# Three edits of order in a tuned encoder layer: earlier last products in a transition, a later copy of v, and P4 ahead of P3

## The chip, the cores and the metric

The kernel runs on one core of a Trainium2 chip. The metric is the device time of one execution in microseconds (us). Engines are named as in the profile: PE is TensorE's matmuls and PEld its weight loads, DVE is VectorE, ACT ScalarE, POOL GpSimd, SP SyncE (which here only issues DMAs).

## What is computed

One layer of an encoder trunk on 1024 tokens of width 1024, in float32: two half-step SwiGLU blocks of hidden width 2816, and between them a mixer that projects into two attentions (a 2-D neighbourhood attention with 8 heads, and a windowed attention with rotary embedding, 8 query heads on 2 key heads), gates their outputs and adds the result.

```python
h = x + 0.5 * swiglu(rms_norm(x, n1), wg1, wu1, wd1)
u = rms_norm(h, nm)
qa, ka, va, qb, kb, vb, ga, gb = split(u @ w_in)
ya = neighbourhood_attention_2d(qa, ka, va, rpb)
yb = windowed_gqa_sink(rope(qb), rope(kb), vb, sink)
h = h + (sigmoid(ga) * (ya @ wa) + sigmoid(gb) * (yb @ wb)) @ wo
h = h + 0.5 * swiglu(rms_norm(h, n2), wg2, wu2, wd2)
y = rms_norm(h, nf)
```

## The kernel before

**Numbers.** Every float32 operand of a big product is split into a high and a low part (`split`, L92: a cast on ACT at L93, a subtraction on DVE at L94), and each product is three matmuls, high by high, high by low, low by high (`mm3`, L145, L147, L149). In the weights' preparation the same two steps stand at L308 (ACT) and L311 (DVE).

**Strassen's scheme.** The big products are done by a seven-product scheme (P1 to P7). Of the right-hand sides, `to_strassen` (L189) turns each of eight token tiles by eight transposes on PE (L138, in `turned`) and puts parts of it into the blocks B11 and B21 (tiles 0 to 3), and T1, T2, B22 (tiles 4 to 7, with sums on DVE at L209 to L215). `strassen_rest` (L221) adds T3 and T4. P4 multiplies T4, and P3 multiplies B22.

**`products` (L233)** runs the seven products of n groups, each in two halves m = 0 and 1, in the order of a list `seq`: P1 and P2 of the first groups, then group by group P5, P6, P7, P3, P4. One product here is 4 column blocks of 3 matmuls, so 12 matmuls. `prep_until` prepares the weights of the product up to eight places ahead. Of group i and half m, P1, P6, P7 and P4 add into one PSUM bank W, P2 goes to X, and P5 and P3 add into Y. After each product the running sum in its bank is read: `after` is called at once behind it. Then `at_end(k)` runs with k, the number of products that are left, and calls whatever is hooked to that k.

**The projections** are `products` with five groups of four chunks of 128 columns (`groups`, L875), 70 products in all, and `store_z` (L879) as `after`: it reads the bank on ACT (L911) where nothing is to be added, and else on DVE (L913), and for P2, P7, P3 and P4 has POOL store the result, to z_d (L891), to g_d (L893), or split to zs_d (L889). The tiles that it writes are a ring of eight in the tensor `fa`. `at_end` runs the hooks of L1034 to L1044, named by the number of products left:

- `rope` (L923), five times at 48, 45, 42, 39 and 36: SP loads a chunk from z_d twice (L931, L934), DVE makes three operations of it (L935 to L937), POOL stores it to zr_d (L938). It takes two tiles `xs`, of which there are two in all.
- `v_b` (L947, at 30) loads v into an `xs` tile; `order_v` (L952, at 28) copies it on ACT in another order into a second `xs` tile (L954); `turn_v` (at 16) transposes it on PE.
- `q_b` and `k_b` (at 7, 6 and 4) split q and k; `gate_first` (at 2) loads the first gate's weights; `keep_u` (L994, at 0) loads the kept part of u (L999) and splits it into the two halves of T4's tile, where the gates behind the projections read it.

**The transition (`transition`, L161)** joins a stage of eight output tiles to the next stage. For each tile t there is `pre(t)`, which for t of 4 and above is `Down.tail(t - 4)` (L623): the last entries of the product P4 of the stage before, 5 entries of 3 matmuls in the first transition and 4 of 3 in the second; then an eviction on DVE (L601) and a store of the tile from SP (L920, L1435). Then `normed` (L116: square on ACT L123, two small steps on POOL L126 and L127, a scaling on DVE L129), then `to_strassen`, then `post`, which from tile 3 on lets the next stage's `products` go on by 30 matmuls. It is called in two halves of four tiles. In the second half the order is: pre(4), pre(5), norm 4; then with tile 4: pre(6), norm 5, turn 4, post; with tile 5: pre(7), norm 6, turn 5, post; and so on. There are two transitions, from the first SwiGLU into the projections (near 580 to 690 us of the trace) and from the mixer into the second SwiGLU (near 1265 to 1330 us).

**What sets the order.** Outside the first stage, which is laid out by hand, the program text gives each instruction a priority by its place, and a planner fixes each engine's order before the run: by its own estimates of durations it gives an engine the first instruction in the text whose inputs and tiles are ready. So an instruction can stand on its engine earlier or later than the text has it, and on the chip each engine then keeps to that fixed order.

**After the projections** attention begins: `scores` (L1268) writes a sink column (L1282) and a softmax (L1283 on DVE, L1286 and L1291 on ACT) into tiles that lie over the ring in `fa`, so it waits until the results there are stored; `turn` transposes them on PE (L1299). Between them PE is filled with the gates' matmuls (`gate`, L1116), which read T4's tile from their fifth block on.

Of the kernel before, what the change touches and what calls it, by code (L numbers as in the profile page):

```python
# [15 lines left out]
P = 128  # L16
# [20 lines left out]
def trunk_kernel(ctx, tc, x, xt, n1, wg1, wu1, wd1, nm, win, rpb, sink, wa, wb, wo,  # L37
# [35 lines left out]
    def new_ar(g, dt=F32R):  # L73
        ar[g] = main.tile([P, 4, 1024], dt, tag=f"ar{g}", bufs=1, name=nm_("ar"))
        return ar[g]
# [28 lines left out]
    def w_cols(w, c0, n=P):  # L104
        return w[:, c0:c0 + n].rearrange("(c p) f -> p c f", p=P)
# [10 lines left out]
    def normed(h, gb, xs=None, parts=1):  # L116

        xs = xs4() if xs is None else xs
        w = D // parts
        cols = [slice(i * w, (i + 1) * w) for i in range(parts)]  # L120
        st = const.tile([P, 4], F32, tag="st", bufs=4, name=nm_("st"))
        for i, c in enumerate(cols):
            nc.scalar.activation(xs[:, c], h[:, c], AF.Square, scale=D ** -0.5, accum_out=st[:, i:i + 1])  # L123
        if parts == 2:
            nc.gpsimd.tensor_tensor(st[:, 0:1], st[:, 0:1], st[:, 1:2], op=ALU.add)
        nc.gpsimd.tensor_scalar(st[:, 0:1], st[:, 0:1], EPS, None, op0=ALU.add)  # L126
        nc.gpsimd.tensor_tensor(st[:, 2:3], st[:, 0:1], nhalf, op=ALU.pow)  # L127
        for c in cols:
            nc.vector.scalar_tensor_tensor(out=xs[:, c], in0=h[:, c], scalar=st[:, 2:3], in1=gb[:, c],  # L129
                                           op0=ALU.mult, op1=ALU.mult)  # L130
        return xs
# [29 lines left out]
    def transition(pre, gain, turn_tile, post, halves=1):  # L161

        h, xs = {}, {}
        n = NTT // halves
        for base in range(0, NTT, n):
            for t in (base, base + 1):
                h[t] = pre(t)
            xs[base] = normed(h.pop(base), gain)
            yield
            for t in range(base, base + n):  # L170
                if t + 2 < base + n:
                    h[t + 2] = pre(t + 2)
                if t + 1 < base + n:
                    xs[t + 1] = normed(h.pop(t + 1), gain)
                turn_tile(t, xs.pop(t))
                if t:
                    post(t - 1)
                yield
        post(NTT - 1)
# [50 lines left out]
    PRODUCTS = ("P1", "P2", "P5", "P6", "P7", "P3", "P4")  # L230
    RIGHT = dict(P1=B11, P2=B21, P6=T2, P5=T1, P7=T3, P3=B22, P4=T4)

    def products(src, n, after, at_end, extra, ring, by_hand=False):  # L233

        seq = [(i, p, m) for i in range(n) for p in PRODUCTS for m in range(2)]  # L240
        early = [(i, p, m) for i in (range(2, 5) if by_hand else range(3)) for p in ("P1", "P2") for m in range(2)]
        if by_hand:
            early = [(i, p, m) for p in ("P2", "P1") for i in range(2) for m in range(2)] + early
# [1 line left out]
        seq = early + [s for s in seq if s not in early]  # L245
# [141 lines left out]
    def behind(prods):  # L387

        run, load_ahead = prods[2:4]

        def post(t):
            if t >= 3:
                drain(run, 10)
            if t in (3, 4):
                load_ahead(t - 2)

        return post

    def hidden(wg, wu, at_end, ring=(8, 9, 10, 11), by_hand=False):
# [16 lines left out]
        def after(i, p, m, bks, snap, sn):  # L416
# [47 lines left out]
            else:  # L464
# [10 lines left out]
                if p != "P3":  # L475
# [10 lines left out]
            yield  # L486

        return products(lambda i, m, half: (wg, wu)[m][i + half * NP], NP, after, at_end, (6, 7),
                        [*ring, *range(8)], by_hand)

# [384 lines left out]
    groups = [[(12, 13), (14, 15)], [(16, 17), (0, 1)], [(4, 5), (8, 9)], [(2, 3), (6, 7)], [(10, 11), (18, 19)]]  # L875
    NG = len(groups)
# [154 lines left out]
    def hook(n, *f):  # L1031
        hooks.setdefault(n, []).append(f)
# [2 lines left out]
        hook(14 * (NG - 1) - 8 - 3 * c, rope, c)  # L1035
    hook(14 * (NG - 2) - 6, rope, 4)
    hook(14 * (NG - 2) - 12, v_b)
    hook(14 * (NG - 2) - 14, order_v)
    hook(14 * (NG - 3) - 12, turn_v)
    hook(7, q_b, 0)  # L1040
    hook(6, k_b)
    hook(4, q_b, 1)
    hook(2, gate_first)
    hook(0, keep_u)  # L1044
    pg = products(lambda i, m, half: w_cols(win[0], groups[i][m][half] * P), NG, store_z, at_end, (2, 3), range(8, 16))
    down.into(transition(down1, gain, to_strassen, behind(pg), 2), pg)
    kept.clear()
    strassen_rest()
# [317 lines left out]
    t = new_ar(2, F32)  # L1366
# [65 lines left out]
    def down2(t):  # L1432
# [3 lines left out]
        return res(t)  # L1436

    merge.into(transition(down2, gain, to_strassen, behind(hg), 2), hg)
    strassen_rest()
    drain(hg[2])  # L1440
# [116 lines left out]
```

## Time and profile before

| | before |
|---|---|
| median of 3 runs | 1935.5 us |
| lowest and highest run | 1934.52 and 1937.35 us |
| span of the profiled execution (its first to its last instruction) | 1934.8 us |
| instructions | 25499 |
| busy: PE | 1922.2 us |
| busy: DVE | 1437.1 us |
| busy: ACT | 943.6 us |
| busy: POOL | 295.5 us |

The page and the trace are of one profiled execution. Beside its span it has no other time of its own; the timed runs are separate ones. A row of the timeline has the start in us from the span's start, the duration in us, the engine, the line, the operation, what it writes and reads, the shape, how often, and in brackets how long the engine had been idle before and what released it. SPq is SP's queue: the rows are DMA issues. Matmuls overlap: each shows 0.39 us, but they follow one another by less.

### The profile page before, as it was taken

How to read it: one execution, taken by the hardware profiler on the slowest of the kernel's cores; microseconds unless marked ns; L12 is line 12 of the kernel's file. 1: busy time of each engine (PE TensorE's matmuls, PEld its weight loads, DVE VectorE, ACT ScalarE, POOL GpSimd, SP SyncE). 2: the span in 40 equal slices, each digit the busy share in tenths (PEclk: the TensorE clock that was granted, in tenths of full speed). 3: DMA queues.
4: the chain of work that ended last, by engine and by line, in shares of the span. 5: the costliest groups of instructions: out<-in, count | busy, mean ns of one | idle time of the engine just before them, and what ended most of it. 6: DMA issues, size and time to landing. Idle time of an engine off the chain costs nothing.

```text
span 1934.8 us, 25499 instructions
## 1 busy us (share of the span) xinstructions
PE 1922.2 (99%) x8956; PEld 1603.1 (83%) x8956; DVE 1437.1 (74%) x2560; ACT 943.6 (49%) x1827; POOL 295.5 (15%) x432
## 2 busy tenths in 40 slices
PE   9999999999999999999999999999999999999998
PEld 7888888888888888888888888878888888888886
DVE  7987765668957788678888857889676566569864
ACT  6532333344446543477877862365333333344453
POOL 0011110013300112211122231010111001005210
PEclk9999999999999999999999999999999999999999
DMA  6344323286234478553458576533423323493341
GB/s 261 100 167 163 129 104 128 86 289 225 88 109 137 159 223 250 185 163 104 116 134 195 184 242 210 169 140 133 147 87 109 126 87 109 140 355 104 112 144 61
DMA packets 151745, 298.70 MB, mean 154 GB/s; under 512 B 14912, under 2 KB 64448, under 8 KB 151616
## 3 DMA queue, kind: packets, MB, share of 16 engines
q1 hardware_dynamic: 123072, 210.53, 33.6%
q0 software_dynamic: 27824, 85.48, 13.3%
q8 instruction: 71, 1.16, 0.3%
q10 hardware_dynamic: 720, 1.05, 0.1%
q14 instruction: 58, 0.48, 0.1%
HBM read 210.50 MB, written 88.27 MB: 154 GB/s over the span
## 4 chain that ended last, share of the span: by engine, by line
PE 88%; issue 7%; POOL 1%; DMA 1%; DVE 1%; ACT 1%; POOLq 0%; SPq 0%; ACTq 0%; DVEq 0%
PE g L149 16%; PE g L147 16%; PE g L145 16%; PE d L149 11%; PE d L147 11%; PE d L145 11%; PE d L1299 2%; PE g L1313 1%; PE g L1318 1%; PE d L1278 1%; PE d L1279 1%; POOL zs_d L889 1%; PE d L138 1%; POOL z_d L891 1%; DMA zr_d<-xs 0%
## 5 line engine op out<-in xcount | busy, mean ns | idle before, releaser
L145 PE MATMUL g<-ar,ws 128*128 128x512 f32 x1128 | 423.1, 395 | 0.6 <-ACT fa L911 0.6
L147 PE MATMUL g<-ar,ws 128*128 128x512 f32 x1128 | 417.2, 390 | 0.9 <-DVE ar L94 0.5
L149 PE MATMUL g<-ar,ws 128*128 128x512 f32 x1128 | 416.1, 390 | 0.2 <-DVE ws L311 0.2
L145 PE MATMUL d<-ar,ws 128*128 128x512 f32 x736 | 282.4, 391 | 0.3 <-ACT ar L810 0.2
L147 PE MATMUL d<-ar,ws 128*128 128x512 f32 x736 | 281.9, 390 | 0.3 <-DVE ar L812 0.3
L149 PE MATMUL d<-ar,ws 128*128 128x512 f32 x736 | 281.6, 390 | 0.5 <-DVE ws L311 0.5
L147 PEld LDWEIGHTS g<-ar,ws 128*128 128x128 f32 x1128 | 211.8, 188 | 46.2 <-DVE ar L94 1.0
L149 PEld LDWEIGHTS g<-ar,ws 128*128 128x128 f32 x1128 | 211.7, 188 | 45.5 <-DVE ws L311 0.7
L145 PEld LDWEIGHTS g<-ar,ws 128*128 128x128 f32 x1128 | 206.4, 188 | 37.8 <-ACT fa L911 1.0
L311 DVE TENSOR_TENSOR ws<-raw,ws 128x512 fp32r<-128x512 f32 x204 | 139.6, 690 | 99.6 <-ACT ws L308 98.8
L308 ACT CAST ws<-raw 128x512 fp32r<-128x512 f32 x204 | 125.1, 620 | 140.6 <-PE g L149 64.4
L145 PEld LDWEIGHTS d<-ar,ws 128*128 128x128 f32 x736 | 138.3, 188 | 29.7 <-ACT ar L810 0.6
L147 PEld LDWEIGHTS d<-ar,ws 128*128 128x128 f32 x736 | 138.4, 188 | 29.6 <-DVE ar L812 0.6
L149 PEld LDWEIGHTS d<-ar,ws 128*128 128x128 f32 x736 | 138.4, 188 | 29.4 <-DVE ws L311 0.7
L93 ACT CAST ws<-raw 128x512 fp32r<-128x512 f32 (+1 forms) x121 | 81.0, 669 | 144.0 <-PE d L149 61.8
L94 DVE TENSOR_TENSOR ws<-raw,ws 128x512 fp32r<-128x512 f32 (+1 forms) x119 | 93.7, 789 | 59.8 <-ACT ws L93 59.3
L414 POOL DMA_DIRECT2D hid<-fx x91 | 49.3, 542 | 431.5 <-DVE fx L474 304.9
L93 ACT CAST ar<-raw 128x512 fp32r<-128x512 f32 (+1 forms) x83 | 56.0, 679 | 94.8 <-PE g L147 55.0
L94 DVE TENSOR_TENSOR ws<-ar,ws 128x512 fp32r<-128x512 f32 x114 | 98.3, 867 | 3.8 <-ACT ws L93 3.7
L145 PE MATMUL g<-ws,ws 128*128 128x512 f32 x232 | 91.0, 392 | 0.0
L149 PE MATMUL g<-ws,ws 128*128 128x512 f32 x232 | 90.5, 390 | 0.0
L147 PE MATMUL g<-ws,ws 128*128 128x512 f32 x232 | 90.3, 389 | 0.0
(313 smaller groups left out, 3607.4 us busy)
## 6 DMA issues: line engine op xcount, KB each, us to landing
raw<-hid SPq DMA_DIRECT2D x70, 512.0 KB
hid<-fx POOLq DMA_DIRECT2D x91, 256.0 KB, 2.4
ar<-in_ffn_w_down_dram SPq DMA_DIRECT2D x32, 512.0 KB
raw<-in_ffn_w_up_dram SPq DMA_DIRECT2D x31, 512.0 KB
raw<-in_ffn_w_gate_dram SPq DMA_DIRECT2D x27, 512.0 KB
raw<-in_w_in_dram SPq DMA_DIRECT2D x27, 512.0 KB
hid<-fa POOLq DMA_DIRECT2D x51, 256.0 KB, 2.7
ar<-zs_d POOLq DMA_DIRECT2D x48, 256.0 KB, 5.3
```

The costliest lines, as they stand in the source:

```text
L93: nc.scalar.copy(dst_hi, src)
L94: (eng or nc.vector).tensor_tensor(dst_lo, src, f32v(dst_hi), op=ALU.subtract)
L138: nc.tensor.transpose(pt[:, c * P:(c + 1) * P], xs[:, (half * 4 + c) * P:(half * 4 + c + 1) * P], ident)
L145: nc.tensor.matmul(b, lhs[0], r[0], start=first, stop=False, **kw)
L147: nc.tensor.matmul(b, lhs[0], r[1], start=False, stop=False, **kw)
L149: nc.tensor.matmul(b, lhs[1], r[0], start=False, stop=last, **kw)
L308: nc.scalar.copy(w[0][:, :512], a)
L311: nc.vector.tensor_tensor(w[0][:, 512:], a, f32v(w[0][:, :512]), op=ALU.subtract)
L414: nc.gpsimd.dma_start(hid[PRODUCTS.index(p), i], src)
L889: nc.gpsimd.dma_start(d[ch * P:(ch + 1) * P, cols], t)
L891: nc.gpsimd.dma_start(z_d[ch * P:(ch + 1) * P, cols], c)
L1299: nc.tensor.transpose(pt[:, i * P:(i + 1) * P], un["pr"][s][:, i * P:(i + 1) * P], ident)
```

## The change

Three edits:

1. In `transition`, in the second half of the tiles, pre(6) and pre(7) both come with tile 4, ahead of norm 5 and of tile 4's transposes; pre(7) came with tile 5. It holds in both transitions.
2. The hook of `order_v` moves from 28 products left to 24.
3. `products` takes the order of the seven as an argument, and the projections have P4 ahead of P3; `keep_u` is hooked to 1 product left in place of 0. The second SwiGLU's and the first one's products keep their order.

```diff
@@ transition
             for t in range(base, base + n):
-                if t + 2 < base + n:
-                    h[t + 2] = pre(t + 2)
+                for k in (t + 2, t + 3) if base and t == base else (t + 2 + (base > 0),):
+                    if k < base + n:
+                        h[k] = pre(k)
                 if t + 1 < base + n:
                     xs[t + 1] = normed(h.pop(t + 1), gain)
                 turn_tile(t, xs.pop(t))
@@ products
-    def products(src, n, after, at_end, extra, ring, by_hand=False):
+    def products(src, n, after, at_end, extra, ring, by_hand=False, order=PRODUCTS):
-        seq = [(i, p, m) for i in range(n) for p in PRODUCTS for m in range(2)]
+        seq = [(i, p, m) for i in range(n) for p in order for m in range(2)]
@@ the projections
-    hook(14 * (NG - 2) - 14, order_v)
+    hook(14 * (NG - 2) - 18, order_v)
-    hook(0, keep_u)
-    pg = products(lambda i, m, half: w_cols(win[0], groups[i][m][half] * P), NG, store_z, at_end, (2, 3), range(8, 16))
+    hook(1, keep_u)
+    pg = products(lambda i, m, half: w_cols(win[0], groups[i][m][half] * P), NG, store_z, at_end, (2, 3), range(8, 16),
+                  order=("P1", "P2", "P5", "P6", "P7", "P4", "P3"))
```

## The prediction

> **What bounds the kernel now.** I read the page's first part, then the waits of TensorE, then the timeline around each of those waits on every engine.
>
> ```profile
> span 1934.8 us, 25499 instructions
> PE 1922.2 (99%) x8956; PEld 1603.1 (83%) x8956; DVE 1437.1 (74%) x2560; ACT 943.6 (49%) x1827; POOL 295.5 (15%) x432
> ```
> ```profile
> PE d L138 <- DVE xs L129: 0.8, 1, 0.8
> PE g L145 <- ACT fa L911: 0.6, 1, 0.6
> PE g L147 <- DVE ar L94: 0.5, 1, 0.5
> PE d L149 <- DVE ws L311: 0.5, 1, 0.5
> ```
>
> The reader is to see how little there is to win. PE is busy for 99% of the span, and the change removes no matmul. These four waits (of 0.8, 0.6, 0.5 and 0.5 us) are all the waits of 0.5 us and more behind the first stage's start, 2.4 us together. The first three lie where the change edits. So the question is whether an edit moves a wait off PE's path without laying a new one on it. A wait costs a little more than the idle time shown: I count from start to start, against the pace of undisturbed matmuls, which the two PE rows of group 0 below give: twelve from 698.67 to 701.39, 0.227 us each.
>
> **Edit 1: tile 7's last products before tile 4's transposes.** This happens in both transitions. In the second one:
>
> ```profile
> 1289.16 0.39 PE L149 MATMUL g<-ws,ws 128*128 128x512 f32 x1
> 1290.35 1.06 PE L138 MATMUL d<-ident,xs 128*128 128x128 f32 x8 [0.80 <-DVE xs L129]
> 1295.59 0.50 PE L149 MATMUL g<-ar,ws 128*128 128x512 f32 x1 [0.24 <-DVE ws L311]
> 1301.43 0.40 PE L149 MATMUL g<-ws,ws 128*128 128x512 f32 x1
> 1315.96 0.50 PE L149 MATMUL d<-ar,ws 128*128 128x512 f32 x1 [0.48 <-DVE ws L311]
> ```
> ```profile
> 1293.65 1.29 DVE L129 SCALAR_TENSOR_TENSOR xs<-fa,st,gain 128x1024 f32<-128x1024 f32 x1 [0.79 <-POOL st L127]
> ```
> ```profile
> 1300.00:1305.00 5.00, 5.00 (x28) 4.21 (x27) 4.99 (x9) 4.87 (x10) 0.51 (x2) 1.00 0.38 126
> ```
>
> The transposes of tile 4 were due at 1289.16 + 0.23 = 1289.39 and began at 1290.35: 0.96 us lost, because tile 4's norm on DVE came late. Tile 7's last products are 4 entries of 3 matmuls, 12 x 0.227 = 2.72 us, and they depend on nothing of the norm. Put in front, they more than fill the gap, and that wait goes. What is late next is DVE. In the window (columns: busy PE, PEld, DVE, ACT, POOL, then clock, DMA) the third busy figure, DVE's, is 4.99 of 5 us, and the wait at 1315.96 already ends with a DVE subtraction of the next stage's weights (L311). Whatever PE gains before 1316 it can keep only as far as DVE gets earlier too. DVE's idle time that this can fill is the 0.79 at 1293.65: the weight tiles come free when tile 7's products have read them, so their conversion can start earlier. I take **-0.8**, nearest to that row. The ends: -1.7 (0.96 + 0.24 + 0.48, if DVE keeps up), and +0.9. The second end because the planner, which orders each engine's instructions by its own estimates, had laid some of tile 7's matmuls among the next stage's (the one at 1301.43 is the last of them); four such fillers gone are 4 x 0.227 = 0.9 us of PE with nothing beside the wait at 1295.59.
>
> Moved with these products go one eviction on DVE and one store of tile 7 on SP's queue, which now precedes weight loads:
>
> ```profile
> 1303.08 0.33 SPq L1435 DMA_DIRECT2D h_d<-fa  x1
> ```
>
> 0.33 us of SP, which waits for nothing there; I cost it at nothing. The first transition:
>
> ```profile
> 642.00 0.39 PE L149 MATMUL g<-ar 128*128 128x512 f32 x1
> 642.23 1.03 PE L138 MATMUL d<-ident,xs 128*128 128x128 f32 x8
> 660.00:670.00 10.00, 10.00 (x54) 8.47 (x53) 10.00 (x17) 7.58 (x14) 1.08 (x2) 1.00 0.49 167
> ```
>
> Here the transposes follow without a gap, so nothing is won. Five entries, 15 x 0.227 = 3.4 us, go ahead of them, and DVE gets tile 4's work 3.4 us later before a stretch in which it is full (10.00 of 10). Idle DVE time later in the tiles covers that; without the cover up to 1 us could return in group 0. Value 0, ends 0 and +1.0.
>
> **Edit 2: P4 ahead of P3.** P6, P7 and P4 add into the same PSUM bank (W); after each, the running sum is read. Between P7 and P4 stood P3, in another bank (Y). Now P4 of half 0 starts one product (2.72 us) after P7 of half 0 ends, and waits until DVE has read that bank. This is the change's added wait, and group 0 shows where it bites:
>
> ```profile
> 698.67 0.39 PE L145 MATMUL d<-ar,ws 128*128 128x512 f32 x1
> 701.39 0.39 PE L145 MATMUL d<-ar,ws 128*128 128x512 f32 x1
> ```
> ```profile
> 696.50 0.69 DVE L315 TENSOR_TENSOR s<-fx 128x512 f32<-128x512 f32 x1 [5.20 <-DMA fx<-in_w_in_dram]
> 699.14 0.69 DVE L913 SCALAR_TENSOR_TENSOR fa<-g,fa 128x512 f32<-128x512 f32 x1
> 703.36 0.68 DVE L913 SCALAR_TENSOR_TENSOR fa<-g,fa 128x512 f32<-128x512 f32 x1
> ```
>
> The PE rows are the starts of the two products behind P7, P3's halves before and P4's after. DVE stands 5.20 us for a weight load and then works off what piled up, so it has read P7's two banks only at 699.14 + 0.69 = 699.83 and 703.36 + 0.68 = 704.04. If all orders stay, P4's first half starts 699.83 - 698.67 = 1.16 us late, the second at 704.04 in place of 701.39 + 1.16 = 702.55, 1.49 late: **2.65 us**. Behind the waiting matmul stands all of PE. Against it: the planner lets a ready product go first where it foresees a wait, as it did with tile 7's matmuls, and P3's inputs are ready. Ends 0 and 2.65; nothing in the trace says which is nearer, so I take the middle, **+1.3**. In the other groups I expect P7's bank to be read in time. In group 3 DVE already stands waiting for P7:
>
> ```profile
> 789.53 0.69 DVE L913 SCALAR_TENSOR_TENSOR fa<-g,fa 128x512 f32<-128x512 f32 x1 [0.58 <-PE g L149]
> ```
>
> 0.69 us of reading fits into the 2.72 of P7's other half. What could break it is a wait of DVE for a rope load, 2.0 us at the longest:
>
> ```profile
> DVE xs L935 <- DMA xs<-z_d: 4.5, 4, 2.0
> ```
>
> 2.0 + 0.69 just fits; with one more operation like the 1.23 us subtraction quoted in edit 4 it is 1.2 over. Value 0, ends 0 and +1.2. P4's own evict is on ACT, P3's on DVE; both only change places, as do the two raw tiles that their preparation frees for SP's loads.
>
> **Edit 3: v's copy.**
>
> ```profile
> 786.43 0.50 PE L145 MATMUL g<-ar,ws 128*128 128x512 f32 x1 [0.56 <-ACT fa L911]
> ```
> ```profile
> 784.84 1.05 ACT L954 COPY xs<-xs 128x1024 f32<-128x1024 f32 x1 [3.26 <-DMA zr_d<-xs]
> 785.79 0.59 ACT L911 ACTIVATE fa<-g 128x512 f32<-128x512 f32 x1
> ```
> ```profile
> 705.53 0.54 POOL L891 DMA_DIRECT2D z_d<-fa  x1 [0.66 <-DVE fa L913]
> ```
> ```profile
> 707.97 0.34 SPq L931 DMA_DIRECT2D xs<-z_d  x1
> ```
>
> ACT stood at v's copy for 3.26 us until the last rope's store had left the tile it writes, then copied for 1.05, and P6's evict behind it came after; P7 on PE lost 0.72 us start to start. The hook's new place alone does little: the copy was already some six products past its hook, held by the store. But P3 of group 0 comes two products later, so the store at 705.53 and the first rope load at 707.97 come 2 x 2.72 = 5.4 us later, and the five ropes run one behind the other through two buffers, so the copy moves to about 784.84 + 5.4 = 790.2. P6's two evicts are then past, and the next evict on ACT is P4's, near 786.43 + 3 x 2.72 = 794.6. **-0.7**; ends -0.7 and, if the copy lands before P6's second evict and waits as long, +1.5.
>
> **Edit 4: T4's split one product earlier.**
>
> ```profile
> 849.02 0.40 PE L147 MATMUL g<-ar,ws 128*128 128x512 f32 x1
> 849.95 0.50 PE L147 MATMUL g<-ar,ws 128*128 128x512 f32 x1 [0.53 <-DVE ar L94]
> 850.75 0.60 PE L1299 MATMUL d<-ident,fa 128*128 128x128 f32 x4
> ```
> ```profile
> 844.84 0.15 DVE L1282 COPY fa<-nsk 128x1 f32<-128x1 f32 x1 [3.78 <-DMA z_d<-fa]
> 845.29 0.15 DVE L1282 COPY fa<-nsk 128x1 f32<-128x1 f32 x1 [0.30 <-DMA g_d<-fa]
> 846.57 0.48 DVE L1283 CUSTOM_DVE_ANT_0 fa<-d,masks,nsk 128x256 f32<-128x256 f32 x1
> 848.67 1.23 DVE L94 TENSOR_TENSOR ar<-raw,ar 128x1024 fp32r<-128x1024 f32 x1
> ```
> ```profile
> 850.00 0.51 ACT L1291 ACTIVATE fa<-fa,rc 128x256 f32<-128x256 f32 x1 [0.87 <-DVE fa L1282]
> ```
>
> P4 was T4's last reader and the last product, so T4 could be refilled only after it. With P3 last, T4 is free 5.4 us earlier, and the split (its last part at 848.67 here) is done before the first gate needs it: 849.95 - 849.02 - 0.23 = 0.7 us won, **-0.7**. The two loads of u that feed it are long issued:
>
> ```profile
> 836.25 1.81 SPq L999 DMA_DIRECT2D raw<-u_d  x2
> ```
>
> so the earlier hook moves ACT's and DVE's parts alone, and no queue of DMAs. The upper end is the rival below.
>
> Sum: -0.8 + 0 + 1.3 + 0 - 0.7 - 0.7 = **-0.9 us**. The profiled execution shows a span of 1934.8; the median of the three runs is 1935.5, 0.7 above it, the margin around the span. So 1934.8 - 0.9 + 0.7 = **1934.6 us**. 0.2% is 3.9 us, about what a measurement of this kernel can tell from no change: I forecast within that.
>
> **Rivals.** *No wait in group 0* (chance 0.22): the planner puts P3's matmuls where P4 would wait. For it speaks that it has done so with tile 7's; against it that its estimate did not foresee DVE's 5.20. Then -2.2, 1933.3.
>
> *First softmax behind P3's store, slower* (0.17): the sink copies of attention's second unit need the buffers of P3's results stored. DVE stood at them until 845.29, ahead of the first unit's softmax at 846.57. P3's store now issues 5.4 us later, less the time its evict had waited. The store's landing:
>
> ```profile
> DMA to landing us min/median/max: 5.4/5.7/6.1
> ```
>
> P3 would end with PE's last projection matmul near 842, its store issue near 843 and land by 849.1. From DVE's release to the first unit's scaled rows took 850.00 + 0.51 - 845.29 = 5.22 us, so 854.3, where PE comes to its transposes at 850.75: +3.6 in place of -0.7. If the two T4 subtractions (1.23 each) now fit into the wait, 851.9, +1.1. It decides as soon as the copies stand ahead of that softmax in DVE's order. I set +2.4 for edit 4: -0.9 + 3.1 = +2.2, 1937.7. A sentence aside: the Trainium skill, page "DMA: Bandwidth & Descriptors", section "Anatomy of one DMA", gives a DMA 2.0 us plus its bytes at 436 GB/s, by which a 256 KB store would land in 2.6 us and this rival would be nearly void; the rows here, with other transfers under way, are twice that, and I go by the rows.
>
> *v's copy blocks another evict* (0.08): edit 3 gives 0 in place of -0.7, 1935.3.
>
> *The waits slow PE's clock, slower* (0.05). PE's granted clock is 1.00 in the windows above, but not everywhere:
>
> ```profile
> 16.00:19.30 3.30, 3.30 (x11) 2.53 (x11) 1.13 (x2) 0.87 (x2) 0.79 (x1) 0.50 1.03 408
> ```
>
> Early in the first stage, behind thin work, it is 0.50 for 3.3 us, half of which is lost: 1.65. Group 0's two waits, 2.65 us within 5.4, could bring the same: 1.35 (the full waits) + 1.65 - 0.9 = +2.1, 1937.6. For it speaks that row; against it that 0.96 us at 1290 left the clock alone. The Trainium skill, page "TensorE: Matmul & The Clock Gate", section "Part 1: The HAM clock gate", lets the clock fall to half after an idle window of about 3.4 us; by that rule waits of 1.16 and 1.49 us cost only themselves, and neither wait of before is long enough to test it.
>
> **How the numbers follow.** Forecast 0.48, rivals 0.22, 0.17, 0.08, 0.05. Low: no wait in group 0 (-2.2) with edit 1 at its end of -1.7 gives -3.1: 1932.4. High: the slower rival at 1937.7 with a little more of group 0's wait: 1938.2. Nearly all cases lie within 0.2%: faster by more than that needs every edit at its good end and something unnamed besides, 0.05; slower by more needs the slower rival with group 0's full wait or the slow clock, 0.11; the same 0.84.
>
> **What would show it.** In the profile after: no wait of L138 on L129 in the second transition, and DVE still full with a PE wait on L311 near 1315; a wait of L145 on DVE's L913 near 700 (up to 1.2 and 1.5); v's copy near 790 with no evict behind it; no wait on L94 near 849, and L1283 ahead of the second unit's L1282. I am wrong if PE waits on L1299 after the projections, or if the planner's order differs far from the edits.

## The result and the profile after

The changed kernel took 1938.87 us (median of 21 runs, 1937.33 to 1940.65), the kernel before 1936.25 us beside it (21 runs, 1934.52 to 1939.16): a ratio of 1.0014, 95% interval 1.0007 to 1.002. So the change costs 2.6 us, where 0.9 us of gain was forecast; the time lies above the range that was given. The profiled execution of the changed kernel has a span of 1937.1 us, 2.3 above that of before.

The page's first part, for the changed kernel:

```profile
span 1937.1 us, 25490 instructions
PE 1921.8 (99%) x8956; PEld 1602.9 (83%) x8956; DVE 1435.4 (74%) x2560; ACT 944.5 (49%) x1827; POOL 293.8 (15%) x432
```

Nothing is to be learned from it: PE is busy for 99% in both, with the same 8956 matmuls. The waits of PE tell more (engine, tile, line, what ended the wait: total, times, longest), from 575 to 1345 us of the changed kernel. Its lines behind `transition` are one further down than those of before, from about 1050 on two.

```profile
PE g L145 <- ACT fa L912: 2.9, 1, 2.9
PE g L145 <- DVE fa L914: 1.5, 2, 1.0
PE d L1301 <- issue: 0.5, 1, 0.5
PE d L145 <- DVE ar L94: 0.2, 1, 0.2
```

All four waits of before are gone or changed. The two of the second transition (L138 on L129, L149 on L311) have vanished, T4's (L147 on L94) too; the one on ACT's evict has grown from 0.6 to 2.9 us, and 1.5 us on DVE's evict are new.

To see what each place is worth, I counted every matmul from start to start and took off the 0.227 us per 512 columns of the undisturbed pace. What is left, in us, by stretch of the span:

| stretch | before | after | after - before |
|---|---|---|---|
| 0 to 640 (first stage, first transition's start) | 11.97 | 10.81 | -1.16 |
| 640 to 700 (first transition, group 0) | 2.27 | 3.97 | +1.71 |
| 700 to 770 (groups 0 to 2) | -0.01 | 0.80 | +0.81 |
| 770 to 830 (groups 3 and 4) | 1.35 | 5.25 | +3.90 |
| 830 to 870 (end of the projections) | 3.01 | 2.21 | -0.80 |
| 870 to 1265 (attention) | 26.41 | 27.11 | +0.70 |
| 1265 to 1345 (second transition) | 6.75 | 3.93 | -2.82 |

The sum is +2.3, the difference of the spans. The first and the sixth row are scatter: these stretches hold the same TensorE work in the same order in every kernel here, and over all fourteen profiles they lie between 10.3 and 12.4 and between 26.1 and 28.3. The first row's scatter has a visible cause: in the profile of before the granted clock was 0.50 for 3.4 us near 16 us, as the prediction shows, and in that of the changed kernel it was 1.00 there. The six profiles with this slow stretch have 11.6 to 12.4 in the row, the eight without it 10.3 to 10.9. The second row has some scatter in it too: five profiles of kernels with the old order there, that of before and four of the experiments, have 2.3 to 3.4 in it, the seven with the new first transition 3.9 to 4.2. The rest I put down to the change.

**Where it went: 770 to 830.** PE and ACT there, from the timeline of the changed kernel (start, duration, engine, line, operation, tiles, shapes; in brackets the idle time before it and what ended that):

```profile
792.86 0.52 PE L145 MATMUL g<-ar,ws 128*128 128x512 f32 x1 [2.91 <-ACT fa L912]
793.60 0.63 PE L149 MATMUL g<-ar,ws 128*128 128x512 f32 x1
794.02 0.63 PE L145 MATMUL g<-ar,ws 128*128 128x512 f32 x1
...
796.58 0.42 PE L145 MATMUL g<-ar,ws 128*128 128x512 f32 x1
```
```profile
784.60 0.60 ACT L912 ACTIVATE fa<-g 128x512 f32<-128x512 f32 x1 [1.68 <-PE g L149]
785.09 0.61 ACT L309 CAST ws<-fx 128x512 fp32r<-128x512 f32 x1
791.26 1.04 ACT L955 COPY xs<-xs 128x1024 f32<-128x1024 f32 x1 [5.56 <-DMA xs<-z_d]
792.21 0.59 ACT L912 ACTIVATE fa<-g 128x512 f32<-128x512 f32 x1
```

Read ACT's rows from top to bottom: P6's first evict, a cast, then v's copy, which waits 5.56 us for its tile, and only behind it P6's second evict. In the kernel before the copy (784.84) stood ahead of both: P6's first evict followed at 785.79, and the second here:

```profile
786.79 0.60 ACT L911 ACTIVATE fa<-g 128x512 f32<-128x512 f32 x1
```

The second evict's bank is the one that P7's second half adds into, so PE stands for 2.91 us. The second thing to see is in PE's starts: from 793.60 on they are 0.42 us apart and not 0.23, until 796.58. The windows of the changed kernel (columns: busy PE, PEld, DVE, ACT, POOL, then PE's granted clock, DMA share, GB/s):

```profile
789.90:792.90 3.00, 0.09 (x2) 0.05 (x1) 0.00 (x0) 1.64 (x3) 0.00 (x0) 1.00 0.22 89
793.20:796.60 3.40, 3.40 (x10) 2.62 (x9) 3.18 (x5) 1.25 (x3) 0.53 (x1) 0.50 0.53 159
796.80:800.20 3.40, 3.40 (x16) 2.78 (x15) 2.07 (x3) 1.25 (x2) 1.35 (x3) 1.00 0.46 142
```

Behind the wait the granted clock is 0.50 for 3.4 us, with 10 matmuls in place of 16, though PE counts as busy all through. Eight starts are 0.2 us late each, 1.6 us. So the copy costs 3.08 (the wait, from start to start) + 1.6 = 4.7 us, less the 0.72 that the wait at 786 had cost before.

**Why the copy is late.** The first rope load and the last rope's store of the changed kernel (SP's queue, POOL):

```profile
711.62 0.34 SPq L932 DMA_DIRECT2D xs<-z_d  x1
783.62 0.53 POOL L939 DMA_DIRECT2D zr_d<-xs  x1 [2.94 <-DVE xs L938]
```

In the kernel before they stand at 707.97 and, by its timeline, at 777.64: the rope chain starts 3.7 us later and ends 6.0 us later.

**The new waits on DVE.** In the first transition and in group 2 of the changed kernel:

```profile
660.98 0.50 PE L145 MATMUL g<-ar,ws 128*128 128x512 f32 x1 [1.01 <-DVE fa L914]
748.84 0.47 PE L145 MATMUL g<-ar,ws 128*128 128x512 f32 x1 [0.45 <-DVE fa L914]
```
```profile
660.24 1.28 DVE L914 SCALAR_TENSOR_TENSOR fa<-g,fa 128x512 f32<-128x512 f32 x2
745.67 1.22 DVE L936 TENSOR_TENSOR xs<-xs,fx 128x1024 f32<-128x1024 f32 x1 [4.05 <-DMA xs<-z_d]
746.81 0.68 DVE L914 SCALAR_TENSOR_TENSOR fa<-d,hs 128x512 f32<-128x512 f32 x1
```

At 660 DVE, without a gap since 648.48, is still at the tiles' work that came to it later (tile 4's third sum, L215, at 651.49; before, at 646.00), and reads group 0's banks late. At 745 it stood 4.05 us for a rope load; before, the longest such wait was 2.0 us.

**What was won.** In the second transition of the changed kernel no wait of PE is left (1265 to 1345 us). The first of the three windows there from 1300 to 1315, and PE at the end of the projections:

```profile
1300.00:1305.00 5.00, 5.00 (x24) 4.09 (x23) 5.00 (x8) 3.88 (x7) 0.54 (x1) 1.00 0.76 285
```
```profile
855.60 0.63 PE L1301 MATMUL d<-ident,fa 128*128 128x128 f32 x4 [0.47 <-issue]
```

DVE's busy time (the third figure) is 5.00 of 5 in all three windows, a little more than before, and PE waits for it nowhere. At the end of the projections the wait for T4's split is gone, and a wait of 0.47 us ahead of the first unit's transposes has come.

### The profile page after: what moved, and what is told of

The parts are those of the page before. It is cut to its first block, busy times and chain, and to the rows that moved or that the text cites. A ratio compares the mean times of both kernels' runs of the same rounds, so it can differ in the third digit from the quotient of the medians.

```text
span 1937.1 us, 25490 instructions
## 1 busy us (share of the span) xinstructions
PE 1921.8 (99%) x8956; PEld 1602.9 (83%) x8956; DVE 1435.4 (74%) x2560; ACT 944.5 (49%) x1827; POOL 293.8 (15%) x432
## 3 DMA queue, kind: packets, MB, share of 16 engines
q8 instruction: 71, 1.16, 0.2%
## 4 chain that ended last, share of the span: by engine, by line
PE 90%; issue 6%; POOL 1%; DVE 1%; ACT 1%; DMA 1%; POOLq 0%; SPq 0%; ACTq 0%; DVEq 0%
PE g L145 17%; PE g L147 17%; PE g L149 17%; PE d L149 11%; PE d L147 11%; PE d L145 11%; PE d L1301 2%; PE g L1320 1%; PE d L1280 1%; PE g L1315 1%; PE d L1281 1%; PE d L138 1%; POOL zs_d L890 1%; POOL z_d L892 0%; DMA fx<-in_xt_dram 0%
## 5 line engine op out<-in xcount | busy, mean ns | idle before, releaser
L147 PE MATMUL g<-ar,ws 128*128 128x512 f32 x1128 | 417.5, 391 | 0.4 <-DVE ar L834 0.4
L149 PE MATMUL g<-ar,ws 128*128 128x512 f32 x1128 | 417.1, 390 | 0.0
L147 PE MATMUL d<-ar,ws 128*128 128x512 f32 x736 | 281.6, 390 | 0.6 <-DVE ar L813 0.6
L149 PE MATMUL d<-ar,ws 128*128 128x512 f32 x736 | 281.1, 389 | 0.1
L147 PEld LDWEIGHTS g<-ar,ws 128*128 128x128 f32 x1128 | 212.1, 188 | 45.2 <-DVE ar L834 0.8
L149 PEld LDWEIGHTS g<-ar,ws 128*128 128x128 f32 x1128 | 212.2, 188 | 45.1
L147 PEld LDWEIGHTS d<-ar,ws 128*128 128x128 f32 x736 | 138.1, 188 | 29.9 <-DVE ar L813 1.2
L149 PEld LDWEIGHTS d<-ar,ws 128*128 128x128 f32 x736 | 138.2, 188 | 29.3 <-DVE ws L312 0.9
L94 DVE TENSOR_TENSOR ws<-raw,ws 128x512 fp32r<-128x512 f32 (+1 forms) x119 | 93.6, 787 | 59.5 <-ACT ws L93 59.0
L94 DVE TENSOR_TENSOR ws<-ar,ws 128x512 fp32r<-128x512 f32 x114 | 98.2, 866 | 5.3 <-ACT ws L93 5.2
L149 PE MATMUL g<-ws,ws 128*128 128x512 f32 x232 | 90.5, 390 | 0.0
L147 PE MATMUL g<-ws,ws 128*128 128x512 f32 x232 | 90.3, 389 | 0.0
```

Of the source, the lines that this page charges most:

```text
L94: (eng or nc.vector).tensor_tensor(dst_lo, src, f32v(dst_hi), op=ALU.subtract)
L147: nc.tensor.matmul(b, lhs[0], r[1], start=False, stop=False, **kw)
L149: nc.tensor.matmul(b, lhs[1], r[0], start=False, stop=last, **kw)
```

## The experiments

**The theory.** P4 ahead of P3 makes P3 of group 0 two products later. P3 writes half of chunk 12, which the first rope loads, so the rope chain runs late, and v's copy with it. The planner had already put the copy, by its own estimate, in front of P6's second evict on ACT; ACT works in order, so the evict waits, PE behind it, and PE's clock falls. **Rivals:** the work that the first transition moves makes the chain late; the hooks do it; the slow clock has another cause.

The hooks could be set aside without a run: the programs with `order_v` hooked at 28 and at 24 products left have the same instructions in the same order on all five engines, with the other edits and without them, and so have those with `keep_u` hooked at 1 and at 0 behind the new order. What is left of the change is the transitions and the order of the products. The ratios below are to the kernel before, timed on the same chip.

### e1: the transitions alone; e2: the order alone

```diff
 e1, against before:
-                if t + 2 < base + n:
-                    h[t + 2] = pre(t + 2)
+                for k in (t + 2, t + 3) if base and t == base else (t + 2 + (base > 0),):
+                    if k < base + n:
+                        h[k] = pre(k)
 e2, against before:
-    hook(0, keep_u)
+    hook(1, keep_u)
-    pg = products(..., range(8, 16))
+    pg = products(..., range(8, 16), order=("P1", "P2", "P5", "P6", "P7", "P4", "P3"))
```

> Edit 1 alone, the orders of products and hooks as before. Theory: the change loses its time through P4 ahead of P3, which brings v's copy ahead of P6's second evict in group 3; so without that order PE has no 2.9 us wait near 790 and no slow clock behind it (granted 0.57 from 792.8 to 796.8 in the changed kernel). What stays of edit 1: the second transition's waits go (from start to start -2.8 us between 1265 and 1345), the first transition costs +1.7 us between 640 and 700 (a wait of about 1.0 us on DVE's evict). Sum -1.1 us against before, about 1935.2. Rival: the work moved in the first transition makes the rope chain late, and with it the copy; then the wait near 790 is here too, 2 us or more, and the sum is +2 to +4.

> P4 ahead of P3 and T4's split earlier, both transitions as before. Theory: the wait behind v's copy (+3.1 us), the slow clock behind it (+1.6), less the wait of before at 786 (-0.7), +0.6 near 749, -0.8 at T4: +3.8 us against before, about 1940. Rival (the first transition makes the copy late): no wait of over 1 us near 790, sum about -1. As to the clock: if any wait of PE of some 2.9 us slows it, it is slow here too for 3.3 us; if that depends on where the wait lies in a window, it may stay at 1.00, and the sum is +2.2.

e1 took 1935.15 us (ratio 0.9997, 0.9989 to 1.0006), e2 1945.24 us (1.0045, 1.0033 to 1.0058). e1 fits the theory: its copy runs at 785.49, and the stretches give +1.73 in the first transition and -2.82 in the second. e2 has the wait and the slow clock, so the order alone brings them, but it is 5.5 us worse than I expected. PE's waits of e2 from 575 to 875 us:

```profile
PE g L145 <- ACT fa L911: 3.6, 1, 3.6
PE g L145 <- DVE fa L913: 1.7, 1, 1.7
...
```
```profile
794.40:797.40 3.00, 3.00 (x8) 2.32 (x9) 2.71 (x5) 1.36 (x3) 0.50 (x1) 0.50 0.62 180
797.40:800.40 3.00, 3.00 (x9) 2.34 (x8) 1.17 (x2) 0.62 (x1) 0.57 (x2) 0.52 0.57 175
```

The wait behind the copy is longer (3.6), the slow clock lasts twice as long (some 6 us, from the two windows), and there is a wait of 1.7 us that the changed kernel does not have: P4 of group 0 on P7's evict (it starts at 700.00), the very wait of the prediction's second term. The transitions had been hiding it.

### e3: the second transition alone, with the new order

```diff
-    def transition(pre, gain, turn_tile, post, halves=1):
+    def transition(pre, gain, turn_tile, post, halves=1, more=False):
-                for k in (t + 2, t + 3) if base and t == base else (t + 2 + (base > 0),):
+                for k in (t + 2, t + 3) if more and base and t == base else (t + 2 + (more and base > 0),):
-    merge.into(transition(down2, gain, to_strassen, behind(hg), 2), hg)
+    merge.into(transition(down2, gain, to_strassen, behind(hg), 2, True), hg)
```

> The whole change, but the first transition keeps its old order; the second has the new one. Theory: the 1.7 us between 640 and 700 go (no wait of L145 on DVE's evict near 661) and all else stays, the 2.9 us behind v's copy too: 1.7 us below the changed kernel, +0.7 against before. Rival: DVE's lateness near 661 is P4's order, and the wait stays: as the changed kernel.

1940.56 us (1.0025, 1.0014 to 1.0035): not 1.7 us below the changed kernel but 1.7 above it. The expectation fell. The wait near 661 is gone as I had it, and P4's wait in group 0 is there instead. PE and DVE of e3, and then DVE of the changed kernel at the same work:

```profile
699.69 0.50 PE L145 MATMUL g<-ar,ws 128*128 128x512 f32 x1 [1.58 <-DVE fa L914]
```
```profile
692.42 0.69 DVE L316 TENSOR_TENSOR s<-fx 128x512 f32<-128x512 f32 x1 [2.26 <-DMA fx<-in_w_in_dram]
...
698.95 0.68 DVE L914 SCALAR_TENSOR_TENSOR fa<-g,fa 128x512 f32<-128x512 f32 x1
```
```profile
690.91 0.69 DVE L316 TENSOR_TENSOR s<-fx 128x512 f32<-128x512 f32 x1 [1.19 <-DMA fx<-in_w_in_dram]
...
697.89 0.68 DVE L914 SCALAR_TENSOR_TENSOR fa<-g,fa 128x512 f32<-128x512 f32 x1
```

PE starts P4 at 699.69, 0.06 us behind the end of the evict (698.95 + 0.68 = 699.63). In the changed kernel the evict is over at 698.57, and P4 is not due before 699.21. The difference begins with the weight load for which DVE stands: the wait of 5.20 us before is 2.26 in e3 and 1.19 in the changed kernel. So the first transition's new order costs up to 1.7 us at 660 and saves as much at 700: a part that costs alone pays in company.

### e4: v's copy on GpSimd

```diff
-        nc.scalar.copy(in_block(r), by_block(mix["vr"]))
+        nc.gpsimd.tensor_copy(in_block(r), by_block(mix["vr"]))
```

> The whole change, but v's copy runs on GpSimd; every other engine's instructions and their order are those of the changed kernel. Theory: ACT no longer stands in front of P6's second evict, so PE's 2.9 us wait near 790 and the slow clock behind it go: 4.7 us below the changed kernel, about -2.1 against before, 1934.1. The copy itself takes some 2.4 us there (as GpSimd's 128x1024 subtractions do) and starts near 791, with v's transposes at 802, so nothing waits for it. Rivals: the slow clock has another cause and stays, then 3.1 below; or P6's second evict is late for its own reasons (PE's bank, ACT's other work), then the wait stays and nothing is won.

1934.10 us (0.9992, 0.9983 to 1.0001), 4.8 below the changed kernel (4.4 when each is set against the kernel before that was timed beside it), where 4.7 was expected. The copy in e4, and the window in which the changed kernel's clock was slow:

```profile
792.52 1.34 POOL L955 COPY xs<-xs 128x1024 f32<-128x1024 f32 x1 [6.79 <-DMA zr_d<-xs]
```
```profile
793.20:796.60 3.40, 3.40 (x17) 2.82 (x16) 3.27 (x5) 1.25 (x2) 1.70 (x3) 1.00 0.33 85
```

The copy is as late as in the changed kernel (792.52), and nobody waits for it. PE works through, and its clock stays at 1.00. With one instruction moved to another engine the wait and the slow clock go together: the slow clock is the wait's doing.

### e5 and e6: the old order, or the new one, in group 0 alone

```diff
 e5, against the changed kernel (e6: "order if i == 0 else PRODUCTS", and keep_u hooked at 0):
-        seq = [(i, p, m) for i in range(n) for p in order for m in range(2)]
+        seq = [(i, p, m) for i in range(n) for p in (order if i else PRODUCTS) for m in range(2)]
```

> The whole change, but the first group keeps P3 ahead of P4; the other four have P4 ahead of P3. Theory: it is group 0's P3 alone that makes the rope chain late, since chunk 12 opens the chain. So the last rope's store issues near 778 as before (783.6 in the changed kernel), v's copy runs near 785, PE waits 0.5 to 0.7 us there and not 2.9, its clock stays at 1.00, and the wait near 749 goes. 4.6 us below the changed kernel, -1.9 against before: 1934. Rival: the late P3 of the other groups delays the chain as well; then the copy comes between 786 and 791 and PE waits between 1 and 3 us.

> The whole change, but P4 ahead of P3 in the first group alone; T4's split is back behind the last product. Theory: everything that group 0's P3 makes late is here: the last rope's store near 784, PE's wait of some 3 us behind v's copy, a granted clock of about half for 3 us or more behind it, and the wait near 749. Only T4's gain goes (0.7 at the end of the projections). So 0.7 above the changed kernel, +3.3 against before: 1939.3. Rival (the other groups' orders make the chain late): the copy near 785 and a time like e1's, 1935.

e5 took 1936.06 us (0.9999, 0.9991 to 1.0008), e6 1938.65 us (1.0007, 0.9997 to 1.0016). The rope chain follows group 0's order in both. The last rope's store issues at 777.69 in e5 and at 783.90 in e6; the copy, in e5 and then in e6:

```profile
784.92 1.05 ACT L955 COPY xs<-xs 128x1024 f32<-128x1024 f32 x1 [3.29 <-DMA zr_d<-xs]
```
```profile
791.43 1.04 ACT L955 COPY xs<-xs 128x1024 f32<-128x1024 f32 x1 [4.55 <-DMA xs<-z_d]
```

With the old order in one group of five the chain is where it was before, and so is the copy; with the new order in that one group both are late. That settles what makes the copy late. The sizes missed: e5's profiled execution, at 1933.69, is the fastest of its eleven, which reach to 1941.66, and the median shows 0.2 us of gain, not 1.9. In e6 the wait was 1.85 us and not 3, because PE came to that place later while the chain did not, and its clock stayed at 1.00 (luck, as the last section shows):

```profile
793.03 0.50 PE L145 MATMUL g<-ar,ws 128*128 128x512 f32 x1 [1.85 <-ACT fa L912]
```
```profile
793.20:796.60 3.40, 3.40 (x16) 2.79 (x17) 3.05 (x5) 1.89 (x4) 0.53 (x1) 1.00 0.54 159
```

### e7: the kernel before, with v's copy on GpSimd

The edit is e4's, made on the kernel before.

> The kernel before with v's copy on GpSimd and nothing else moved. It measures what the third edit could win: PE's wait of 0.56 us at 786 on P6's evict goes, 0.7 us from start to start, and nothing takes its place; the copy runs about 1.3 us behind the last rope's store. If P6's evict is late there for another reason, the wait stays.

One run, 1934.33 us, too few to compare times. The wait at 786 is gone and nothing has come in its place: the stretch from 770 to 830 falls from 1.35 to 0.46 us, 0.9 and not 0.7.

### e8: the parts that won, together

e3's transition, e5's order and e4's copy in one kernel.

> The parts that won, together: the second transition's new order alone, P4 ahead of P3 in groups 1 to 4 with T4's split earlier, and v's copy on GpSimd. Theory, place by place against before: second transition -2.8, P6's evict at 786 -0.7, T4 -0.8, the first transition and group 0 as before: -4.3 us, 1931.6, below both kernels. Rival: with the copy gone from ACT another late operation takes its place in group 3, or the shorter way makes the first softmax late (a wait on L1300 of 0.5 or more): -3 or less.

1934.76 us (0.9993, 0.9984 to 1.0001): 1.5 us of gain and not 4.3. By the stretches -2.8 in the second transition and -0.9 at 770 to 830 came as expected. T4's stretch won 0.14 in place of 0.8. From 640 to 770, in the main in the old order, it lost 1.1, with waits of 0.2 us near 656 and of 0.5 us near 677, and the attention stretch lay 1.3 higher; both I count as scatter, and the interval of 3 us is too wide to say more. The size is the rival's; of its two causes the trace shows a wait of 0.4 us ahead of the first unit's transposes, and none in group 3.

### e9: the second transition and the copy alone; e12: with the last group's order

```diff
 e9 is the kernel before with e3's transition and e4's copy; e12, against e9:
-        seq = [(i, p, m) for i in range(n) for p in PRODUCTS for m in range(2)]
+        seq = [(i, p, m) for i in range(n) for p in (order if i == n - 1 else PRODUCTS) for m in range(2)]
-    hook(0, keep_u)
+    hook(1, keep_u)
```

> The kernel before with two things alone: the second transition's new order and v's copy on GpSimd; the products keep P3 ahead of P4, the first transition its old order, T4's split its old place. Theory, by places: second transition -2.8, P6's evict at 786 -0.9 (e7 measured 0.9 between 770 and 830), nothing added: -3.7, 1932.6, below both kernels and the best of all. Rival: what these waits give up comes back elsewhere (DVE or a load late in group 0, the attention stages): -2 or less.

> As e9 (second transition's new order, v's copy on GpSimd), and the last group alone has P4 ahead of P3, with T4's split a product earlier. It measures the fourth edit by itself. Theory: the waits on T4's split at the end of the projections (e9: 0.65 and 0.70 us from start to start near 848 and 849) go, a wait of 0.5 to 0.6 before the first unit's transposes (L1301) comes in their place, as in every kernel here with that order; net -0.8 to -0.1 against e9 between 830 and 870, and nothing elsewhere: 1932.2 to 1932.9. Rival: P3's late store holds the sink copies and with them a softmax; then +1 or more there.

e9 took 1932.97 us (0.9983, 0.9975 to 0.9992), e12 1932.64 us (0.9983, 0.9974 to 0.9992). Both are faster than the kernel before, by 0.17%, and by some 6 us than the changed kernel. e9 lies 3.25 us below the kernel before, where 3.7 was expected; e12 is within what was expected of it. The two can't be told apart in time. Between 830 and 870 e12 lies 0.9 us below e9 (2.69 against 3.62): that is the fourth edit by itself, in one pair of profiles. PE's waits of e12, from 575 to 1345 us:

```profile
PE d L145 <- ACT ws L309: 0.3, 1, 0.3
PE d L1301 <- issue: 0.2, 1, 0.2
```

### e10: the ropes in another order

```diff
-    for c in range(4):
-        hook(14 * (NG - 1) - 8 - 3 * c, rope, c)
+    for j, c in enumerate((1, 3, 0, 2)):
+        hook(14 * (NG - 1) - 8 - 3 * j, rope, c)
```

> The whole change, v's copy on ACT as there, but the ropes run in the order of chunks 13, 15, 12, 14, 16 in place of 12, 13, 14, 15, 16: chunk 13 needs P4 of group 0 and not P3, and P4 is now the earlier one. Theory (the chain's first chunk sets when v's copy can run): the first rope load issues near 705 (711.6 in the changed kernel), the last rope's store near 778 or earlier, v's copy at 785 or earlier, PE's wait there at most 0.7 us, clock at 1.00: 3.9 to 4.7 us below the changed kernel, -1.3 to -2.1 against before. Rival: the chain is bound by its loads and by DVE in the groups behind, not by its start; then the copy comes after 788 and PE waits 1 us or more.

1936.66 us (1.0005, 0.9996 to 1.0015), 2.2 below the changed kernel, where 3.9 to 4.7 were expected. The chain did as the theory had it: its last store issues at 779.27, the copy runs at 784.90, and PE does not wait there. But DVE now stands 4.16 us for a rope load in group 2, with an evict behind it, and PE waits there:

```profile
754.08 1.23 DVE L936 TENSOR_TENSOR xs<-xs,fx 128x1024 f32<-128x1024 f32 x1 [4.16 <-DMA xs<-z_d]
755.23 0.68 DVE L914 SCALAR_TENSOR_TENSOR fa<-g,fa 128x512 f32<-128x512 f32 x1
```
```profile
756.06 0.47 PE L145 MATMUL g<-ar,ws 128*128 128x512 f32 x1 [2.17 <-DVE fa L914]
```

It is the same mechanism on another engine: an instruction that waits for a rope's transfer stands in front of an evict. The clock was 1.00 behind this wait of 2.17 us.

### e11: half of the copy on ACT

```diff
-        nc.scalar.copy(in_block(r), by_block(mix["vr"]))
+        for f, s in ((nc.scalar.copy, slice(0, 4)), (nc.gpsimd.tensor_copy, slice(4, 8))):
+            f(in_block(r)[:, s], by_block(mix["vr"])[:, s])
```

> The whole change, but ACT copies only half of v's tile, GpSimd the other half; all else as in the changed kernel. P6's second evict comes 0.5 us earlier, so PE's wait near 790 is about 2.4 us. It tells how long a wait must be to slow PE's clock: 1.85 us (e6) left it at 1.00, 2.91, 3.29 and 3.59 us did not. If 2.4 is enough, ten matmuls behind it run at about 0.43 us each, 1.6 us lost; if not, the time is 2.1 us below the changed kernel.

One run, 1939.73 us. The wait was shorter than meant, 1.86 us, that of e6 to a hundredth, and this time the clock fell, to 0.50 (the window is in the last section). PE in e11:

```profile
792.76 0.50 PE L145 MATMUL g<-ar,ws 128*128 128x512 f32 x1 [1.86 <-ACT fa L912]
...
793.58 0.40 PE L145 MATMUL g<-ar,ws 128*128 128x512 f32 x1
793.81 0.54 PE L147 MATMUL g<-ar,ws 128*128 128x512 f32 x1
794.15 0.63 PE L149 MATMUL g<-ar,ws 128*128 128x512 f32 x1
```

## Why the prediction was wrong, point by point

- **Edit 3, v's copy (-0.7): the step that failed.** "P6's two evicts are then past" took the copy's place on ACT as given by the time when it could run. Its place is given by the planner's order; the copy moved 6.4 us in time, but only one evict in the order. The row that I quoted showed it already: ACT stood 3.26 us at the copy, in front of an evict, because the planner had thought it ready earlier. The end of +1.5 and the rival at 0 named this case and under-priced it: the wait was 3.08 and brought 1.6 of slow clock. The stretch lost 3.9 us where 0.7 of gain was forecast. That is more than the whole difference between forecast and result; e4 and e5 show it.
- **The base.** 1935.5 was the median of three runs; 21 runs give 1936.25. So 0.75 of the 4.3 us between the time forecast and the time measured is the base, and the change itself was off by 3.5 (+2.6 against -0.9). The 0.7 that the prediction calls the margin around the span is not one: an execution that has both figures, the changed kernel's profiled one, took 1938.85 us with a span of 1937.1, so 1.75 more.
- **The rival of the slow clock** was put on group 0's waits, with a chance of 0.05. Its price (1.65, measured 1.6) was right and its place was not: it came behind the copy's wait, to which I had given no clock at all.
- **Edit 2, P4 in group 0 (+1.3).** The changed kernel has no such wait. e2 and e3, without the first transition's new order, do: 1.86 and 1.74 us from start to start, within the bounds. The size was fair; what failed was costing the edits one by one. The first transition moved the weight load that my working took as fixed.
- **Edit 2, other groups (0, ends 0 and +1.2).** +0.8, most of it at 748.84: the load wait that I held to 2.0 us was 4.05. The chain now runs among other transfers; that this makes the load slower is not shown.
- **Edit 1, first transition (0, ends 0 and +1.0).** +1.7 by these two profiles, 0.5 to 1.9 by all: the mechanism as named, the size at or beyond its end. With the new order of the products it is repaid at 700.
- **Edit 1, second transition (-0.8, ends -1.7 and +0.9).** -2.8. I held DVE to be the next bound since it was busy for 4.99 of 5 us. It is as full after, and nobody waits. Full is not late: between 1285 and 1290 us its busy time went from 3.62 to 4.83 us, and by 1300 it had worked 13.17 us in place of 12.45; that this start is what kept it ahead is read off the windows and was not tried by itself. No window of a full engine says how much slack its consumers have. The end of -1.7 was also added up too small: it took one wait from start to start (0.96) and two as idle time (0.24, 0.48), where from start to start the three cost 0.96, 0.41 and 0.70, together 2.07; the rest lies in slower steps behind and between them.
- **Edit 4 (-0.7).** Its mechanism and about its size were right: -0.8 here and -0.9 in e12. Over all profiles the stretch has a mean of 3.1 with the old order at the end (five) and of 2.5 with the new one (nine), so -0.5, the new wait of 0.2 to 0.8 us before the first unit's transposes included. It comes from the order and not from the hook.
- **First softmax behind P3's store.** It did not come: the sink copies stayed behind the first softmax in DVE's order in the changed kernel.

What stays open: the scatter of e5 and e10, whose runs spread over 8 and 11 us while those of the kernel before spread over 4 to 5. A slow clock that comes in some executions only would add 1.6 us each time, too little for this alone, and e5's profile has no wait over 1.0 us; a profile shows one execution, so the cause is not shown.

## What to carry to other kernels

In a program whose order is fixed ahead, ask of each waiting instruction what stands behind it on its engine, and take its place from the order and not from the time at which it can run: when its input gets later, it stays where it is and everything behind it waits. An operation that waits for a long chain of transfers belongs on an engine that holds nothing that TensorE needs; here one copy, moved to GpSimd, was worth 4.8 us. And price edits together before adding them up: the first transition's cost of up to 1.7 us and group 0's wait of 1.7 us cancelled each other, and each part alone misled.

## What the runs showed of the hardware

A wait of TensorE costs more than itself when the clock falls behind it. The waits, with the clock from each profile's windows (the third column is explained below):

| kernel | PE's wait, us | idle time in each window of the grid, us | granted clock behind it |
|---|---|---|---|
| e2, at 700 | 1.69 | 1.69 | 1.00 |
| e6 | 1.85 | 0.85 and 0.99 | 1.00 |
| e11 | 1.86 | 1.86 | 0.50 for 3.41 us |
| e10 | 2.17 | 0.87 and 1.30 | 1.00 |
| after | 2.91 | 2.91 | 0.50 for 3.41 us |
| e3 | 3.29 | 2.96 and 0.33 | 0.50 for 3.41 us |
| e2, at 794 | 3.59 | 2.86 and 0.73 | 0.50 for 6.83 us |

Waits of nearly one length, 1.85 and 1.86 us, came out both ways, so length alone does not decide. The grid of the third column does most of it. In each of the fourteen traces the granted clock changes only at times that lie whole multiples of 3.413 us apart: in e11 at 15.68, 19.09, 793.92 and 797.33, in the changed kernel at 4.72, 793.20 and 796.62. So each execution has a grid of windows of 3.413 us, and where it lies against the kernel differs from one to the next. Here are windows of that grid, of e11 and then of e6 (the first figure behind the length is PE's busy time, the one behind POOL's the clock):

```profile
790.51:793.92 3.41, 1.55 (x7) 0.96 (x6) 0.67 (x2) 2.14 (x4) 0.61 (x1) 1.00 0.25 91
793.92:797.33 3.41, 3.41 (x10) 2.62 (x9) 2.51 (x5) 0.62 (x1) 1.07 (x2) 0.50 0.69 208
```
```profile
788.62:792.03 3.41, 2.56 (x12) 1.79 (x10) 0.00 (x0) 0.60 (x1) 0.00 (x0) 1.00 0.77 312
792.03:795.45 3.42, 2.42 (x11) 2.01 (x12) 1.90 (x4) 2.58 (x5) 0.00 (x0) 1.00 0.47 139
```

e11's wait lies whole in one window, which keeps its pace to its end, so that the matmuls go on for about 1 us at the full pace, and the next window is slow. e6's wait is cut in two by an edge, and neither half slows anything: that its clock stayed at 1.00 was luck. The slow stretch near 16 us obeys the same cut. Some 2 us with nothing but thin matmuls (128x1 each) come shortly before that time in all fourteen profiles; in the seven in which an edge cuts them, at most 1.5 us in a window, the clock stays at 1.00, and of the seven in which one window holds 1.93 us or more of them it falls in six. No sharp limit comes out of this: in the seventh of these, e1, 1.94 us left the clock alone, and so did 1.86 and 1.93 us of idle time in one window at the very end of e3 and e10. Why e2's clock stayed slow for two windows, no run separates.

The Trainium skill, page "TensorE: Matmul & The Clock Gate", section "Part 1: The HAM clock gate", has the clock halved after an idle window of about 3.4 us, with windows that run on their own and not from the kernel's start. The runs agree with the free windows and with their length. They do not agree with a whole idle window: 1.86 us was enough in e11. In the prediction I had let that rule pass as the reason why short waits cost only themselves.

GpSimd copied the 128x1024 tile in 1.34 us in e4, where ACT took 1.04 in the changed kernel; from its 128x1024 subtractions, 2.45 us each, I had expected 2.4.
